# Evacuations in place, without temporaries, and attention masks made during the pooling stage

## The chip, the cores and the metric

The kernel runs on one core of a Trainium2 chip. The metric is the device time of one launch in microseconds (us). TensorE is called PE (its weight load PEld), VectorE DVE, ScalarE ACT, GpSimd POOL and SyncE SP. L12 is line 12 of the kernel whose profile is read; the same step has another line number in the changed kernel, since lines fall away.

## The reference

A decoder trunk of two layers on 256 tokens of width 2048, in float32. Layer 0 mixes tokens by causal means over windows of 2, 4, 8 and 16; layer 1 by causal attention with 16 heads, whose keys and values come from the stream after layer 0. Each mixer is followed by a gated feed-forward part with a causal convolution of width 3, and every part ends in a residual sum and a layer norm:

```python
def layer(h, mixer):
    h = layer_norm(ALPHA * h + mixer(h), ln1_g, ln1_b)
    u = h @ w_up                              # 2048 -> gate and value, D_FF each
    u = causal_conv3(u, conv_w, conv_b)
    g = silu(gate(u)) * value(u)
    return layer_norm(ALPHA * h + g @ w_down, ln2_g, ln2_b)
```

The three dilated branches of the attention (windows 128, 512 and 2048, strides 1, 4 and 16) see each other's keys several times. The kernel therefore weighs each pair of tokens with the number of branches that hold it. That count depends on the distance of the tokens alone: it is the mask `cnt`, and `negm` is a large negative number where the count is zero.

## The kernel before

Weights are streamed once. The work is cut into units, one for each weight block of 512 x 512, and a list gives their order. `run_units` goes through the list: before the matmuls of a unit it loads the raw block of the unit five further on (SP, `rawp`, three buffers) and splits the block three units further on into a high part `wh` (ACT cast, L82) and a low part `wl` (DVE subtraction, L83), each with four buffers. PE then multiplies wh and wl with the high and low parts of the activations, which stand for a product in float32. Blocks of the down projection are split in another way (L96, L97, L103 to L109) for a scheme of seven products with sums and differences of blocks; its outputs are added onto `ht` by DVE or by accumulating transfers that POOL issues (L271), and are transposed (L814) and moved on SP (L804).

The order of the instructions of each engine is that in which the code is written; `later(n, fn)` puts fn behind the matmuls n units on. So a step that waits holds up all that stands behind it on its engine.

An accumulator of PE has two halves of 256 columns, for the high and the low part of the activations, which have to be added. `evac` does that for an up group of four blocks of 128 channels: ACT copies the right half of a block to a temporary `ut` (L578; tag t1, three buffers), and DVE adds the left half and the temporary into `u` (L579). `u` comes from the tag t4 of the same pool, with four buffers, in which the convolution also keeps its results `c` and `a`. `qk_post` does the same for q and k of four heads (L978, L979; temporary `qt`, two buffers). Where the input of the layer norm is still folded into the product, `norm_evac` is used instead (L442 to L449), also with a temporary. The pooling stage has its own evacuation (L471, L473), which copies into the destination and adds in place there.

The stages follow each other in the list: pooling with its feed-forward part, then the attention with its own. The pools of temporaries `ffn0`, `attn` and `ffn1` stand in sequence. `masks` makes one of two blocks of `cnt` and `negm` (L1171 to L1178 on DVE, an iota on POOL, and for the first block two ACT copies, L1182). It runs 7 and 8 units into the attention stage, into buffers of the pool `attn`, with scratch from the tag t1, which the temporaries of q use too.

Of the kernel before, what the change touches and what calls it, by code (L numbers as in the profile page):

```python
# [17 lines left out]
T = 256  # L18
P = 128
# [9 lines left out]
NEG = -1e30  # L29
# [3 lines left out]
def trunk(ctx: ExitStack, tc: tile.TileContext, x, pool_w_in, pool_w_grp, pool_scale, pool_w_out,  # L33
# [86 lines left out]
    def later(n, fn):  # L120
        if n == 0:
            fn()
        else:
            pending.append([n, fn])
# [176 lines left out]
    ones4 = const.tile([P, P], F32R, name="ones4")  # L301
    epst = const.tile([P, 1], F32, name="epst")
    inv = const.tile([P, 1, 16], F32, name="inv")

    xsrcs = [lambda j=j: XC[j] for j in range(4)]
    psrcs = [lambda j=j: XP[j] for j in range(4)]
# [241 lines left out]
    def ffn(lay):  # L548
# [15 lines left out]
            return u  # L564

        def evac(ps, nb, mode):
            fp = pools["ffn"]
            u = pads()

            def tmp():  # L570
                return fp.tile([P, T], F32, name="ut", tag="t1", bufs=3)

            if mode == "x":
                norm_evac(ps, nb, tmp, lambda m: u[:, m, 2:])
                return u
            for m in range(nb):
                t = tmp()
                A.copy(t, ps[m][:, T:])  # L578
                V.tensor_tensor(u[:, m, 2:], ps[m][:, :T], t, OP.add)  # L579
            return u  # L580

        def conv(u, blk0, nb, then, quick=False):
# [378 lines left out]
    def qk_post(nm, hq):  # L961
        def post(ps):
            later(2 if hq == 0 and nm == "k" else 0, lambda: evac(ps))

        def evac(ps):
            ap = pools["attn"]
            o = ap.tile([P, 4, T], F32, name=nm, tag=nm)
            qk[nm] = o

            def tmp():  # L970
                return ap.tile([P, T], F32, name="qt", tag="t1", bufs=2)

            if hq == 0 and nm == "k":
                norm_evac(ps, 4, tmp, lambda m: o[:, m, :])
            else:
                for m in range(4):
                    t = tmp()
                    A.copy(t, ps[m][:, T:])  # L978
                    V.tensor_tensor(o[:, m, :], ps[m][:, :T], t, OP.add)  # L979
            if nm == "q":  # L980
                later(2, lambda: scores(hq, range(0, 2)))
                later(3, lambda: scores(hq, range(2, 4)))
                if hq < 3:
                    later(4, lambda: blocks(hq, (0, 1)))
                    later(7, lambda: blocks(hq, (2, 3)))
        return post

    def scores(hq, ms):
        ap = pools["attn"]
        for m in ms:  # L990
            ps = bank("s")
            q, k = qk["q"][:, m, :], qk["k"][:, m, :]
            PE.matmul(ps[:, 0:P], q[:, :P], k[:, :P], start=True, stop=True)
            PE.matmul(ps[:, P:3 * P], q[:, P:], k, start=True, stop=True)
            if m % 2 == 0:
                two = ap.tile([P, 2, 3, P], F32, name="p", tag="p", bufs=2)
            s = two[:, m % 2]
            sf, nf, cf = (t.rearrange("p a b -> p (a b)") for t in (s, ST["negm"], ST["cnt"]))
            V.scalar_tensor_tensor(sf, ps[:, :3 * P], scale, nf, op0=OP.mult, op1=OP.add)
            mx = ap.tile([P, 6], F32, name="mx", tag="mx", bufs=4)  # L1000
            parts = ((0, slice(0, P)), (1, slice(P, 3 * P)))
            for t, sl in parts:
                V.tensor_reduce(mx[:, t:t + 1], sf[:, sl], AX.X, OP.max)
            V.tensor_scalar(mx[:, 2:4], mx[:, 0:2], -1.0, None, op0=OP.mult)
            for t, sl in parts:
                A.activation(sf[:, sl], sf[:, sl], AF.Exp, bias=mx[:, 2 + t:3 + t])
            pr[hq, m] = (s, mx, two)
        for m in ms:
            s, mx, _ = pr[hq, m]
            sf, cf = (t.rearrange("p a b -> p (a b)") for t in (s, ST["cnt"]))  # L1010
            for t, sl in parts:
                V.scalar_tensor_tensor(sf[:, sl], sf[:, sl], 1.0, cf[:, sl], op0=OP.mult, op1=OP.mult,
                                       accum_out=mx[:, 4 + t:5 + t])
            V.reciprocal(mx[:, 0:2], mx[:, 4:6])
            for t, sl in parts:
                V.tensor_scalar(sf[:, sl], sf[:, sl], mx[:, t:t + 1], None, op0=OP.mult)
# [95 lines left out]
    with tc.tile_pool(name="pool", bufs=1) as pp:  # L1112
# [17 lines left out]
        def late_consts(l):  # L1130
# [16 lines left out]
            A.copy(t, ps.rearrange("p (j c) -> p j c", j=4)[:, :, :2 * NF])  # L1147
            cvec.append(t)

        later(2, lambda: late_consts(0))  # L1150
        later(4, lambda: late_consts(1))

# [4 lines left out]
        run_units(marks[1])  # L1157
    with tc.tile_pool(name="attn", bufs=1) as ap:
        pools["attn"] = ap
        for nm in ("cnt", "negm"):  # L1160
            ST[nm] = ap.tile([P, 3, P], F32, name=nm)

        def masks(i):
            two = ap.tile([P, 2, P], F32, name="dist", tag="t1", bufs=2)
            dist, fm = two[:, 0], two[:, 1]
            nc.gpsimd.iota(dist, pattern=[[-1, P]], base=P * (i == 1), channel_multiplier=1,
                           allow_small_or_imprecise_dtypes=True)
# [3 lines left out]
            V.tensor_copy(idist, dist)  # L1171
            V.tensor_scalar(cn, dist, float(P), None, op0=OP.is_le)
            for dil in (4, 16):
                V.tensor_scalar(im, idist, dil - 1, None, op0=OP.bitwise_and)
                V.tensor_copy(fm, im)
                V.scalar_tensor_tensor(cn, fm, 0.0, cn, op0=OP.is_equal, op1=OP.add)
            V.scalar_tensor_tensor(cn, dist, 0.0, cn, op0=OP.is_ge, op1=OP.mult)
            V.tensor_scalar(ST["negm"][:, i, :], cn, 0.0, NEG, op0=OP.is_equal, op1=OP.mult)  # L1178

            if i == 0:  # L1180
                for nm in ("cnt", "negm"):
                    A.copy(ST[nm][:, 2, :], ST[nm][:, 0, :])  # L1182

        for i in range(2):
# [34 lines left out]
```

## Time and profile before

| | us |
|---|---|
| median of 3 runs | 2051.32 (2048.59 to 2051.43) |
| the profiled execution | 2051.56 |
| span of the profiled execution | 2049.8 |
| PE busy | 2025.5 |
| DVE busy | 1684.2 |
| ACT busy | 1259.6 |
| POOL busy | 74.9 |

The profile is of one execution. The span goes from its first to its last instruction, and the launch's own time is 1.8 us more. Busy time is that in which an engine has at least one instruction under way. The idle time of an engine that is not the bottleneck costs nothing in itself; it counts where another engine waits for what comes late from it. All columns and groups below are in us unless marked ns.

### The profile page before, as it was taken

To read this page: it belongs to the slowest core of one execution; us is meant where nothing else is said; L and a number is where in the kernel's file an instruction comes from. 1 tells how busy PE (TensorE), PEld (TensorE's weight loads), DVE (VectorE), ACT (ScalarE), POOL (GpSimd) and SP (SyncE) were. 2 spreads that over 40 slices of the span, in tenths; PEclk is the share of its full clock that TensorE was granted. 3 is DMA by queue.
4 is the path that set the end of the run, shared out by engine and by line. 5 is a ranking of instruction groups with operands and counts; after the bars stand their busy time and mean duration, and the time that the engine had idled before them with its cause. 6 is when DMAs were issued, how large, how long until landed. Compare 5 with 4: busy or idle time off the path is not lost. (4 is left out here: it accounts for less than half of the span.)

```text
span 2049.8 us, 31251 instructions
## 1 busy us (share of the span) xinstructions
PE 2025.5 (99%) x12532; PEld 1809.4 (88%) x12532; DVE 1684.2 (82%) x2010; ACT 1259.6 (61%) x1691; POOL 74.9 (4%) x111
## 2 busy tenths in 40 slices
PE   9999999999999999999999999999999999999998
PEld 8899988899899989889888888998899988889987
DVE  6759876998889898889856657787889888989989
ACT  6545687666756686657544444477666677667663
POOL 2000000000000101000000000000001000100000
PEclk9999999999999999999999999999999999999999
DMA  8655467667656657775566554557666756666565
GB/s 263 213 190 186 169 211 202 191 194 235 196 190 201 202 190 210 211 231 170 167 218 191 173 180 165 185 185 221 187 199 185 227 181 208 205 216 197 184 206 185
DMA packets 278305, 405.92 MB, mean 198 GB/s; under 512 B 80414, under 2 KB 95668, under 8 KB 277904
## 3 DMA queue, kind: packets, MB, share of 16 engines
q1 hardware_dynamic: 266144, 389.72, 57.5%
q0 software_dynamic: 11584, 13.55, 4.4%
q8 instruction: 98, 1.61, 0.3%
q10 hardware_dynamic: 432, 0.66, 0.1%
q14 instruction: 47, 0.39, 0.1%
HBM read 380.01 MB, written 2.10 MB: 186 GB/s over the span
## 5 line engine op out<-in xcount | busy, mean ns | idle before, releaser
L165 PE MATMUL acc<-xc,wh 128*128 128x512 f32 x3264 | 1152.8, 396 | 1.2 <-DVE o L1064 1.2
L166 PE MATMUL acc<-xc,wl 128*128 128x256 f32 x3264 | 917.3, 281 | 5.3 <-DVE wl L83 5.1
L83 DVE TENSOR_TENSOR wl<-raw,wh 128x2048 fp32r<-128x2048 f32 (+2 forms) x318 | 687.5, 2168 | 259.1 <-ACT wh L82 258.7
L165 PEld LDWEIGHTS acc<-xc,wh 128*128 128x128 f32 x3264 | 615.9, 189 | 144.4 <-DVE o L1064 1.9
L82 ACT CAST wh<-raw 128x2048 fp32r<-128x2048 f32 (+2 forms) x318 | 573.7, 1810 | 201.2 <-PE acc L165 108.4
L166 PEld LDWEIGHTS acc<-xc,wl 128*128 128x128 f32 x3264 | 615.4, 189 | 9.2 <-DVE wl L83 8.5
L96 ACT CAST wh<-raw 128x1024 fp32r<-128x1024 f32 x116 | 121.9, 1053 | 156.8 <-DVE raw L107 133.4
L97 DVE TENSOR_TENSOR wl<-raw,wh 128x1024 fp32r<-128x1024 f32 x116 | 138.4, 1221 | 0.0
L103 ACT CAST wh<-raw 128x1024 fp32r<-128x1024 f32 x116 | 90.7, 832 | 35.6 <-DMA raw<-in_ffn_w_down_dram 21.3
L106 DVE TENSOR_TENSOR wl<-raw,wh 128x1024 fp32r<-128x1024 f32 x116 | 105.7, 952 | 2.6 <-ACT wh L103 2.2
L587 ACT ACTIVATE c<-u,cv 128x256 f32<-128x256 f32 x172 | 89.5, 593 | 24.6 <-DVE f L650 8.5
L578 ACT COPY ut<-acc 128x256 f32<-128x256 f32 x164 | 53.1, 372 | 81.6 <-DVE u L579 58.6
L228 PE MATMUL t<-wl,g 128*128 128x256 f32 x344 | 97.0, 282 | 0.0
L227 PE MATMUL t<-wh,g 128*128 128x256 f32 x344 | 97.0, 282 | 0.0
L229 PE MATMUL t<-wh,g 128*128 128x256 f32 x344 | 96.7, 281 | 0.0
L228 PE MATMUL s<-wl,xs 128*128 128x256 f32 x308 | 86.9, 282 | 3.8 <-DVE wl L97 3.8
L229 PE MATMUL s<-wh,xs 128*128 128x256 f32 x308 | 86.4, 280 | 0.0
L227 PE MATMUL s<-wh,xs 128*128 128x256 f32 x308 | 86.3, 280 | 0.0
L271 POOL DMA_DIRECT2D ht<-w x24 | 20.3, 847 | 1770.6 <-ACT wh L103 1034.8
L592 ACT ACTIVATE a<-u,cv 128x256 f32<-128x256 f32 x172 | 73.6, 501 | 12.3 <-DVE g L660 6.5
L592 ACT ACTIVATE u<-u,cv 128x256 f32<-128x256 f32 x172 | 73.5, 500 | 0.0
L109 DVE TENSOR_TENSOR raw<-raw 128x1024 f32<-128x1024 f32 x58 | 71.0, 1225 | 2.0
(278 smaller groups left out, 3433.8 us busy)
## 6 DMA issues: line engine op xcount, KB each, us to landing
raw<-in_ffn_w_up_dram SPq DMA_DIRECT2D x160, 1024.0 KB, 4.9
raw<-in_ffn_w_down_dram SPq DMA_DIRECT2D x80, 1024.0 KB, 5.1
raw<-in_pool_w_out_dram SPq DMA_DIRECT2D x16, 1024.0 KB, 5.0
raw<-in_shared_w_k_dram SPq DMA_DIRECT2D x16, 1024.0 KB, 5.1
raw<-in_attn_w_q_dram SPq DMA_DIRECT2D x16, 1024.0 KB, 5.4
raw<-in_shared_w_v_dram SPq DMA_DIRECT2D x16, 1024.0 KB, 5.6
raw<-in_attn_w_o_dram SPq DMA_DIRECT2D x16, 1024.0 KB, 5.0
raw<-in_pool_w_in_dram SPq DMA_DIRECT2D x12, 1024.0 KB, 5.5
```

The source lines that it names most:

```text
L82: A.copy(wh[i][:, s], r[:, s])
L83: V.tensor_tensor(wl[i][:, s], r[:, s], wh[i][:, s].bitcast(F32), OP.subtract)
L96: A.copy(h[:, :, n], r[:, :, n])
L97: V.tensor_tensor(l[:, :, n], r[:, :, n], h[:, :, n].bitcast(F32), OP.subtract)
L103: A.copy(h[:, k, n], r[:, k, n])
L106: V.tensor_tensor(l[:, k, n], r[:, k, n], h[:, k, n].bitcast(F32), OP.subtract)
L165: PE.matmul(ps[m], h[:, k, c], q[:, k, :, :T], start=st, stop=False)
L166: PE.matmul(ps[m][:, :T], l[:, k, c], q[:, k, 0, :T], start=False, stop=sp and not shifted)
L227: PE.matmul(to, xh, h[:, k, n], start=opens and kk == 0, stop=False)
L228: PE.matmul(to, xh, l[:, k, n], start=False, stop=False)
L229: PE.matmul(to, xl, h[:, k, n], start=False, stop=ends and kk == 1)
L592: A.activation(to[:, m, :], u[:, m, i:i + T], AF.Copy, scale=cv[:, i, j:j + 1])
```

## The change

The temporaries of `evac`, of q and k and of `norm_evac` are dropped: ACT copies the right half of the accumulator straight into the destination, and DVE adds the left half to it in place; in `norm_evac` DVE and ACT work in the destination. `cnt` and `negm` move to the pool of constants, and `masks` runs 9 and 10 units into the pooling stage, with scratch from two tags of the pool `lnp` that are free there.

```diff
@@ -301,6 +301,8 @@
     ones4 = const.tile([P, P], F32R, name="ones4")
     epst = const.tile([P, 1], F32, name="epst")
     inv = const.tile([P, 1, 16], F32, name="inv")
+    cnt = const.tile([P, 3, P], F32, name="cnt")
+    negm = const.tile([P, 3, P], F32, name="negm")
 
     xsrcs = [lambda j=j: XC[j] for j in range(4)]
     psrcs = [lambda j=j: XP[j] for j in range(4)]
@@ -436,17 +438,17 @@
         later(5, lambda: lo(3))
 
 
-    def norm_evac(ps, nb, tmp, dst):
+    def norm_evac(ps, nb, dst):
         wgb = lnp.tile([P, 4, 2], F32, name="wgb", tag="wgb", bufs=2)
         for m in range(nb):
             A.copy(wgb[:, m, :], ps[m][:, T:XW])
         for m0 in range(0, nb, 2):
-            ts = [(m, tmp()) for m in range(m0, min(nb, m0 + 2))]
+            ts = [(m, dst(m)) for m in range(m0, min(nb, m0 + 2))]
             for m, t in ts:
                 V.tensor_tensor(t, ps[m][:, :T], ST["rs"], OP.mult)
             for m, t in ts:
                 V.scalar_tensor_tensor(t, ST["mr"], wgb[:, m, 0:1], t, op0=OP.mult, op1=OP.subtract)
-                A.activation(dst(m), t, AF.Identity, scale=-1.0, bias=wgb[:, m, 1:2])
+                A.activation(t, t, AF.Identity, scale=-1.0, bias=wgb[:, m, 1:2])
 
 
     def turns(mark, n, nb):
@@ -564,19 +566,14 @@
             return u
 
         def evac(ps, nb, mode):
-            fp = pools["ffn"]
             u = pads()
 
-            def tmp():
-                return fp.tile([P, T], F32, name="ut", tag="t1", bufs=3)
-
             if mode == "x":
-                norm_evac(ps, nb, tmp, lambda m: u[:, m, 2:])
+                norm_evac(ps, nb, lambda m: u[:, m, 2:])
                 return u
             for m in range(nb):
-                t = tmp()
-                A.copy(t, ps[m][:, T:])
-                V.tensor_tensor(u[:, m, 2:], ps[m][:, :T], t, OP.add)
+                A.copy(u[:, m, 2:], ps[m][:, T:])
+                V.tensor_tensor(u[:, m, 2:], u[:, m, 2:], ps[m][:, :T], OP.add)
             return u
 
         def conv(u, blk0, nb, then, quick=False):
@@ -967,16 +964,12 @@
             o = ap.tile([P, 4, T], F32, name=nm, tag=nm)
             qk[nm] = o
 
-            def tmp():
-                return ap.tile([P, T], F32, name="qt", tag="t1", bufs=2)
-
             if hq == 0 and nm == "k":
-                norm_evac(ps, 4, tmp, lambda m: o[:, m, :])
+                norm_evac(ps, 4, lambda m: o[:, m, :])
             else:
                 for m in range(4):
-                    t = tmp()
-                    A.copy(t, ps[m][:, T:])
-                    V.tensor_tensor(o[:, m, :], ps[m][:, :T], t, OP.add)
+                    A.copy(o[:, m, :], ps[m][:, T:])
+                    V.tensor_tensor(o[:, m, :], o[:, m, :], ps[m][:, :T], OP.add)
             if nm == "q":
                 later(2, lambda: scores(hq, range(0, 2)))
                 later(3, lambda: scores(hq, range(2, 4)))
@@ -995,7 +988,7 @@
             if m % 2 == 0:
                 two = ap.tile([P, 2, 3, P], F32, name="p", tag="p", bufs=2)
             s = two[:, m % 2]
-            sf, nf, cf = (t.rearrange("p a b -> p (a b)") for t in (s, ST["negm"], ST["cnt"]))
+            sf, nf, cf = (t.rearrange("p a b -> p (a b)") for t in (s, negm, cnt))
             V.scalar_tensor_tensor(sf, ps[:, :3 * P], scale, nf, op0=OP.mult, op1=OP.add)
             mx = ap.tile([P, 6], F32, name="mx", tag="mx", bufs=4)
             parts = ((0, slice(0, P)), (1, slice(P, 3 * P)))
@@ -1007,7 +1000,7 @@
             pr[hq, m] = (s, mx, two)
         for m in ms:
             s, mx, _ = pr[hq, m]
-            sf, cf = (t.rearrange("p a b -> p (a b)") for t in (s, ST["cnt"]))
+            sf, cf = (t.rearrange("p a b -> p (a b)") for t in (s, cnt))
             for t, sl in parts:
                 V.scalar_tensor_tensor(sf[:, sl], sf[:, sl], 1.0, cf[:, sl], op0=OP.mult, op1=OP.mult,
                                        accum_out=mx[:, 4 + t:5 + t])
@@ -1147,27 +1140,14 @@
             A.copy(t, ps.rearrange("p (j c) -> p j c", j=4)[:, :, :2 * NF])
             cvec.append(t)
 
-        later(2, lambda: late_consts(0))
-        later(4, lambda: late_consts(1))
-
-        run_units(marks[0])
-    with tc.tile_pool(name="ffn0", bufs=4) as fp:
-        pools["ffn"] = fp
-
-        run_units(marks[1])
-    with tc.tile_pool(name="attn", bufs=1) as ap:
-        pools["attn"] = ap
-        for nm in ("cnt", "negm"):
-            ST[nm] = ap.tile([P, 3, P], F32, name=nm)
-
         def masks(i):
-            two = ap.tile([P, 2, P], F32, name="dist", tag="t1", bufs=2)
-            dist, fm = two[:, 0], two[:, 1]
+            both = lnp.tile([P, 4, T], F32, name="dist", tag="sq")
+            dist, fm = (both[:, j, :P] for j in range(2))
+            two = lnp.tile([P, 2, T], I32, name="idist", tag="fold2")
+            idist, im = two[:, 0, :P], two[:, 1, :P]
             nc.gpsimd.iota(dist, pattern=[[-1, P]], base=P * (i == 1), channel_multiplier=1,
                            allow_small_or_imprecise_dtypes=True)
-            itwo = ap.tile([P, 2, P], I32, name="idist", tag="t1", bufs=2)
-            idist, im = itwo[:, 0], itwo[:, 1]
-            cn = ST["cnt"][:, i, :]
+            cn = cnt[:, i, :]
             V.tensor_copy(idist, dist)
             V.tensor_scalar(cn, dist, float(P), None, op0=OP.is_le)
             for dil in (4, 16):
@@ -1175,14 +1155,23 @@
                 V.tensor_copy(fm, im)
                 V.scalar_tensor_tensor(cn, fm, 0.0, cn, op0=OP.is_equal, op1=OP.add)
             V.scalar_tensor_tensor(cn, dist, 0.0, cn, op0=OP.is_ge, op1=OP.mult)
-            V.tensor_scalar(ST["negm"][:, i, :], cn, 0.0, NEG, op0=OP.is_equal, op1=OP.mult)
-
+            V.tensor_scalar(negm[:, i, :], cn, 0.0, NEG, op0=OP.is_equal, op1=OP.mult)
             if i == 0:
-                for nm in ("cnt", "negm"):
-                    A.copy(ST[nm][:, 2, :], ST[nm][:, 0, :])
+                for t in (cnt, negm):
+                    A.copy(t[:, 2, :], t[:, 0, :])
 
         for i in range(2):
-            later(7 + i, lambda i=i: masks(i))
+            later(9 + i, lambda i=i: masks(i))
+        later(2, lambda: late_consts(0))
+        later(4, lambda: late_consts(1))
+
+        run_units(marks[0])
+    with tc.tile_pool(name="ffn0", bufs=4) as fp:
+        pools["ffn"] = fp
+
+        run_units(marks[1])
+    with tc.tile_pool(name="attn", bufs=1) as ap:
+        pools["attn"] = ap
         run_units(marks[2])
     with tc.tile_pool(name="ffn1", bufs=4) as fp:
         pools["ffn"] = fp
```

Where the steps land is seen in the order of instructions. First an evacuation in layer 0, on DVE and on ACT, before (u is the destination, acc the accumulator, raw the loaded block; numbers tell buffers of a name apart):

```order
L83 TENSOR_TENSOR wl_4501<-raw_4437,wh_4500 128x2048
L563 MEMSET u 128x4x2
L579 TENSOR_TENSOR u<-acc,ut 128x256 x4
L83 TENSOR_TENSOR wl_4551<-raw_4466,wh_4550 128x2048
L104 TENSOR_TENSOR raw_4498<-raw_4498 128x2x256
```

```order
L82 CAST wh_4500<-raw_4437 128x2048
L578 COPY ut<-acc 128x256 x4
L82 CAST wh_4550<-raw_4466 128x2048
L587 ACTIVATE c<-u,cv_590 128x256 x4
L103 CAST wh_4579<-raw_4498 128x4x256
```

And the same place with the change, DVE and ACT:

```order
L83 TENSOR_TENSOR wl_4499<-raw_4435,wh_4498 128x2048
L565 MEMSET u 128x4x2
L576 TENSOR_TENSOR u<-u,acc 128x256 x4
L83 TENSOR_TENSOR wl_4545<-raw_4464,wh_4544 128x2048
L104 TENSOR_TENSOR raw_4496<-raw_4496 128x2x256
```

```order
L82 CAST wh_4498<-raw_4435 128x2048
L575 COPY u<-acc 128x256 x4
L82 CAST wh_4544<-raw_4464 128x2048
L584 ACTIVATE c<-u,cv_592 128x256 x4
L103 CAST wh_4573<-raw_4496 128x4x256
```

Nothing has moved here; operands have changed. Second, DVE in the pooling stage ahead of the adds (pb is their destination) that end the second of its groups, before:

```order
L83 TENSOR_TENSOR wl_815<-raw_685,wh_814 128x2048
L83 TENSOR_TENSOR wl_857<-raw_742,wh_856 128x2048
L83 TENSOR_TENSOR wl_895<-raw_812,wh_894 128x2048
L83 TENSOR_TENSOR wl_933<-raw_854,wh_932 128x2048
L473 TENSOR_TENSOR pb_420<-pb_420,acc 128x256 x4
```

and with the change, the end of the first block of masks and what follows up to the second:

```order
L1156 SCALAR_TENSOR_TENSOR cnt<-dist,cnt 128x128
L1157 SCALAR_TENSOR_TENSOR cnt<-dist,cnt 128x128
L1158 TENSOR_SCALAR negm<-cnt 128x128
L83 TENSOR_TENSOR wl_950<-raw_856,wh_949 128x2048
L1151 CAST idist<-dist 128x128
L1152 TENSOR_SCALAR cnt<-dist 128x128
L1154 TENSOR_SCALAR idist<-idist 128x128
```

Ten steps now stand ahead of the fourth wl of the four, and ten between it and the adds. Third, DVE in the attention stage ahead of the first q, before, the end of the second block of masks:

```order
L1176 SCALAR_TENSOR_TENSOR cnt<-dist,cnt 128x128
L1177 SCALAR_TENSOR_TENSOR cnt<-dist,cnt 128x128
L1178 TENSOR_SCALAR negm<-cnt 128x128
L979 TENSOR_TENSOR q<-acc,qt 128x256 x4
L83 TENSOR_TENSOR wl_9725<-raw_9605,wh_9724 128x2048
```

and with the change:

```order
L450 SCALAR_TENSOR_TENSOR k<-rm,wgb,k 128x256 x2
L83 TENSOR_TENSOR wl_9546<-raw_9437,wh_9545 128x2048
L83 TENSOR_TENSOR wl_9584<-raw_9486,wh_9583 128x2048
L972 TENSOR_TENSOR q<-q,acc 128x256 x4
L83 TENSOR_TENSOR wl_9631<-raw_9543,wh_9630 128x2048
```

The add of q now follows straight behind two wl. The order of PE and of SP is the same in both kernels; on POOL the two iotas stand ahead of all accumulating transfers.

More of the change, by code (lines that the diff above doesn't have):

```diff
@@ L1148, in late_consts, with masks @@
             cvec.append(t)
+        def masks(i):
+            both = lnp.tile([P, 4, T], F32, name="dist", tag="sq")
+            dist, fm = (both[:, j, :P] for j in range(2))
+            two = lnp.tile([P, 2, T], I32, name="idist", tag="fold2")
+            idist, im = two[:, 0, :P], two[:, 1, :P]
+            nc.gpsimd.iota(dist, pattern=[[-1, P]], base=P * (i == 1), channel_multiplier=1,
+                           allow_small_or_imprecise_dtypes=True)
+            cn = cnt[:, i, :]
+            V.tensor_copy(idist, dist)
+            V.tensor_scalar(cn, dist, float(P), None, op0=OP.is_le)
+            for dil in (4, 16):
+                V.tensor_scalar(im, idist, dil - 1, None, op0=OP.bitwise_and)
+                V.tensor_copy(fm, im)
+                V.scalar_tensor_tensor(cn, fm, 0.0, cn, op0=OP.is_equal, op1=OP.add)
+            V.scalar_tensor_tensor(cn, dist, 0.0, cn, op0=OP.is_ge, op1=OP.mult)
+            V.tensor_scalar(negm[:, i, :], cn, 0.0, NEG, op0=OP.is_equal, op1=OP.mult)
+            if i == 0:
+                for t in (cnt, negm):
+                    A.copy(t[:, 2, :], t[:, 0, :])
+        for i in range(2):
+            later(9 + i, lambda i=i: masks(i))
         later(2, lambda: late_consts(0))
@@ L1159, in trunk @@
         pools["attn"] = ap
-        for nm in ("cnt", "negm"):
-            ST[nm] = ap.tile([P, 3, P], F32, name=nm)
-        def masks(i):
-            two = ap.tile([P, 2, P], F32, name="dist", tag="t1", bufs=2)
-            dist, fm = two[:, 0], two[:, 1]
-            nc.gpsimd.iota(dist, pattern=[[-1, P]], base=P * (i == 1), channel_multiplier=1,
-                           allow_small_or_imprecise_dtypes=True)
-            itwo = ap.tile([P, 2, P], I32, name="idist", tag="t1", bufs=2)
-            idist, im = itwo[:, 0], itwo[:, 1]
-            cn = ST["cnt"][:, i, :]
[L1171 to L1180, printed above, removed]
-                for nm in ("cnt", "negm"):
-                    A.copy(ST[nm][:, 2, :], ST[nm][:, 0, :])
-        for i in range(2):
-            later(7 + i, lambda i=i: masks(i))
         run_units(marks[2])
```

## The prediction

> **What bounds the kernel now.** I read the head of the page first, then the waits of TensorE (PE), then its waits in windows, and then the timeline of the two engines that prepare its operands.
>
> ```profile
> span 2049.8 us, 31251 instructions
> PE 2025.5 (99%) x12532; PEld 1809.4 (88%) x12532; DVE 1684.2 (82%) x2010; ACT 1259.6 (61%) x1691; POOL 74.9 (4%) x111
> ```
>
> PE is busy for 99% of the span. The change leaves its instructions and their order alone, so all that can be won is the time in which PE stands still. The waits of PE over the whole span (total, times, longest, in us) show how much that is, and for whom PE waits:
>
> ```profile
> PE acc L166 <- DVE wl L83: 5.1, 8, 2.0
> PE s L228 <- DVE wl L97: 3.8, 4, 1.5
> PE t L229 <- DVE xs3Q L660: 1.9, 1, 1.9
> PE acc L168 <- ACT wh L82: 1.9, 1, 1.9
> PE acc L165 <- DVE o L1064: 1.2, 1, 1.2
> ```
>
> Two rows, 8.9 us together, are waits for wl, the low half of a weight block, which VectorE (DVE) makes from the raw block and the high half wh that ScalarE (ACT) casts before it. The wait for L82 (1.9) stands in the first 10 us, which the change does not touch. The other waits for wl are placed by windows: the first row is 600 to 780 us, the next two 780 to 870, then one of 1700 to 1900 and two of 1900 to 1980; the L1064 row above is the only one of 1000 to 1080.
>
> ```profile
> PE acc L166 <- DVE wl L83: 1.3, 3, 0.7
> PE s L228 <- DVE wl L97: 2.6, 2, 1.5
> PE acc L166 <- DVE wl L83: 2.4, 2, 2.0
> PE acc L166 <- DVE wl L83: 1.0, 2, 0.8
> PE s L228 <- DVE wl L97: 0.9, 1, 0.9
> PE acc L166 <- DVE wl L83: 0.5, 1, 0.5
> ```
>
> So wl comes late in two stretches, the end of each layer's feed-forward part: 6.3 us in layer 0, 2.4 us in layer 1. What delays DVE there? The waits of ACT hold one suspect, and the timeline around 658 us shows one evacuation of an up group (start, duration, engine, line; in brackets the idle time before and its releaser; first ACT, then DVE):
>
> ```profile
> ACT ut L578 <- DVE u L579: 58.6, 27, 3.8
> ```
>
> ```profile
> 657.88 0.91 ACT L578 COPY ut<-acc 128x256 f32<-128x256 f32 x3
> 660.74 0.38 ACT L578 COPY ut<-acc 128x256 f32<-128x256 f32 x1 [1.95 <-DVE u L579]
> 661.01 1.92 ACT L82 CAST wh<-raw 128x2048 fp32r<-128x2048 f32 x1
> ...
> 658.02 2.29 DVE L83 TENSOR_TENSOR wl<-raw,wh 128x2048 fp32r<-128x2048 f32 x1 [0.58 <-ACT wh L82]
> 660.24 0.41 DVE L579 TENSOR_TENSOR u<-acc,ut 128x256 f32<-128x256 f32 x1
> 660.57 1.07 DVE L579 TENSOR_TENSOR u<-acc,ut 128x256 f32<-128x256 f32 x3
> 662.96 2.29 DVE L83 TENSOR_TENSOR wl<-raw,wh 128x2048 fp32r<-128x2048 f32 x1 [1.32 <-ACT wh L82]
> ```
>
> ACT makes three copies and stops: there are three buffers ut and four blocks. The fourth copy waits until DVE has done its first add (660.65), and DVE gets to that only after a wl of 2.29 us. Behind the fourth copy stands the next L82 cast, which ends at 662.93, and DVE, done with its adds at 661.64, stands idle for 1.32 us until that cast is there. The loop costs DVE 1.32 us an evacuation, where DVE is what PE waits for.
>
> **The change part by part.** Evacuation of up groups. Without ut the four ACT copies go straight into four parts of u and need none of the adds. They would run from 657.88 for 4 x 0.30 = 1.2 us, the cast behind them from 659.1 to 661.0, and DVE would find it ready at 661.64. So each evacuation of four blocks gives DVE back the bracket of the wl behind it. The add itself now reads u and the accumulator rather than the accumulator and ut. That form is in the trace, in the pooling stage (L473; by line and form: total, mean ns):
>
> ```profile
> L579 DVE TENSOR_TENSOR u<-acc,ut 128x256 f32<-128x256 f32 x164 | 58.0, 414 | 1.8 <-ACT ut L578 1.8
> L473 DVE TENSOR_TENSOR pb<-pb,acc 128x256 f32<-128x256 f32 x12 | 4.5, 414 | 1.9 <-ACT pb L471 1.9
> ```
>
> Both take 414 ns, so the add costs the same. How far do the brackets reach PE? The same bracket stands behind these evacuations before the stalls of layer 0, the first three in full:
>
> ```profile
> 736.31 2.29 DVE L83 TENSOR_TENSOR wl<-raw,wh 128x2048 fp32r<-128x2048 f32 x1 [1.31 <-ACT wh L82]
> 752.52 2.29 DVE L83 TENSOR_TENSOR wl<-raw,wh 128x2048 fp32r<-128x2048 f32 x1 [1.31 <-ACT wh L82]
> 784.60 2.29 DVE L83 TENSOR_TENSOR wl<-raw,wh 128x2048 fp32r<-128x2048 f32 x1 [1.31 <-ACT wh L82]
> 817.38 1.76 DVE L83 TENSOR_TENSOR wl<-raw,wh 128x1536 fp32r<-128x1536 f32 x1 [0.88 <-ACT wh L82]
> 819.83 1.25 DVE L814 STREAM_TRANSPOSE hb<-ht 128x1024 f32<-128x1024 f32 x1 [0.70 <-DMA ht<-u]
> ```
>
> With the one at 662.96 that is 4 x 1.31 = 5.2 us of DVE time against 6.3 us of stalls. The last row shows why the one at 817.38 counts nothing: the next DVE step waits for a transfer anyhow. I take 5.2 us for layer 0. The lower bound is the 1.3 us of 600 to 780, which lie straight behind evacuations; the upper one is all 6.3. In layer 1 the evacuations behind 1740 us are of the same kind, with more brackets than stalls, so I take the 2.4 us of stalls there; the last of them hang on a cast that waits for PE,
>
> ```profile
> 1958.90 2.24 ACT L96 CAST wh<-raw 128x1024 fp32r<-128x1024 f32 x2 [0.97 <-PE acc L165]
> ```
>
> so that no more than 0.97 us can come at that place, and the 0.9 and 0.5 there may not both go: 2.3 us, with 1.0 as the lower bound. The upper bound adds the 1.9 us of L229 (a later step of the same chain) and what follows it, the PE clock (windows: length, busy of PE, PEld, DVE, ACT, POOL, then granted clock, DMA share, GB/s; first 3 us behind a stall of 2.0 us in layer 0, then 3 us behind that of 1.9):
>
> ```profile
> 835.00:838.00 3.00, 3.00 (x19) 2.58 (x18) 2.52 (x4) 1.72 (x3) 0.00 (x0) 1.00 0.86 292
> 1985.10:1988.10 3.00, 3.00 (x16) 3.00 (x15) 3.00 (x6) 2.78 (x6) 0.00 (x0) 0.50 0.36 88
> ```
>
> Behind the second, PE ran at half clock for 3 us, which costs 1.5 us; behind the first it did not. The Trainium skill's page "TensorE: Matmul & The Clock Gate" (section "What's actually happening") gives half clock only after an idle window of about 3.4 us; by that rule a stall of 1.9 us would cost nothing more, and the upper bound would be 1.5 us smaller. The row at 1985 speaks against it. Upper bound of layer 1: 2.4 + 1.9 + 1.5 = 5.8 us.
>
> Evacuation of q and k. Same edit, four blocks and two buffers. Here the masks of the attention stage make it worse: they stand on DVE ahead of the first q evacuation (first and last step of one of two blocks of ten; the copy and the cast that wait behind it; what PE's only stall here hangs on):
>
> ```profile
> 987.07 0.22 DVE L1171 CAST idist<-dist 128x128 int32<-128x128 f32 x1
> 989.24 0.23 DVE L1178 TENSOR_SCALAR negm<-cnt 128x128 f32<-128x128 f32 x1
> 995.43 0.37 ACT L978 COPY qt<-acc 128x256 f32<-128x256 f32 x1 [3.83 <-DVE dist L1175]
> 997.27 3.71 ACT L82 CAST wh<-raw 128x2048 fp32r<-128x2048 f32 x2
> 1035.92 0.74 DVE L1064 TENSOR_TENSOR o<-o 128x256 fp32r<-128x256 f32 x2
> ```
>
> Each block is 2.4 us (987.07 to 989.47). Without them and without the wait of 3.83 us, DVE and ACT are 3 to 4 us earlier at 1000; the stall of 1.2 us at 1036 hangs on the DVE step of the last row, 36 us on, behind softmax, transfers and transposes. I take all 1.2 us; bounds 0 and 1.2.
>
> Masks in the pooling stage. The 20 DVE steps (4.8 us), two ACT copies and two POOL iotas come back there. On POOL the iotas stand behind the small constant loads and ahead of all accumulating transfers, which start hundreds of us later, so nothing queues behind them. On DVE the first block falls between two wl, the second between a wl and the adds that free the banks of the next unit (DVE, ACT, then PE's opening of that unit):
>
> ```profile
> 82.78 2.29 DVE L83 TENSOR_TENSOR wl<-raw,wh 128x2048 fp32r<-128x2048 f32 x1 [3.28 <-ACT wh L82]
> 87.00 0.42 DVE L473 TENSOR_TENSOR pb<-pb,acc 128x256 f32<-128x256 f32 x1 [0.93 <-ACT pb L471]
> ...
> 80.84 1.91 ACT L82 CAST wh<-raw 128x2048 fp32r<-128x2048 f32 x1 [3.66 <-PE acc L165]
> ...
> 92.11 0.40 PE L165 MATMUL acc<-xc,wh 128*128 128x512 f32 x1
> ```
>
> The first block fits into the 3.28 us in which DVE idles, but the two ACT copies wait for its end (82.78 - 3.28 + 2.4 = 81.9) and push the cast from 80.84 to about 82.1, and so the wl from 82.78 to about 84.0. It ends at 86.3, the second block at 88.7, and the last of four adds at about 90.4 at the latest instead of 87.4. PE opens the unit at 92.11: 1.7 us of cover is left, and the cost is 0. Gone, the cover would cost some tenths of a us. Bounds: 0 and 4.8 us, if all steps lay on the path.
>
> Sum: 5.2 + 2.3 + 1.2 - 0 = 8.7 us. The profiled execution took 2051.56 us, 0.24 above the median 2051.32, so 2042.9 of its kind and 2042.6 as a median.
>
> **The rivals.** A, only stalls that lie straight behind evacuations go. From 780 us on the path runs through loads of down blocks and through transfers (the 0.70 before L814 at 819.83 is one such wait); if those set the pace, an earlier DVE only waits longer for them. Left are 1.3 in layer 0, 1.0 in layer 1 and 1.2 at 1036: 3.5 us, 2047.8. For it speaks that row; against it that DVE at 784.60 waits for ACT and not for a transfer.
>
> B, nothing comes of it: DVE ahead by a few us is stopped by ACT casts that wait for PE to free a wh buffer (3.66 us before 80.84 is such a wait), and every stall forms again; the 1.2 at 1036 goes or stays. 2050.1 to 2051.3.
>
> C, slower: the wait moves from ut to u. ACT's first copy now needs a whole free u of the ring t4, which also holds c, a and what the gate makes, four buffers in all; before, only DVE's add needed it, behind work of DVE's own. If the ring is freed by the DVE convolution steps, the copy stalls in place, and the L82 behind it. Two such steps of some 1.2 us (the transposing step of 1.25 at 819.83 has the same 1024 elements a row) cost 2.5 us where 1.31 is won: 1.2 us lost at each of the 7 evacuations with DVE on the path in layer 0 (624 to 817), 8.4 us in all: 2059.7. It decides as soon as the copy waits for over 1.31 us. The order of instructions speaks against it: of 41 evacuations the first copy gets a new wait in only four. The Trainium skill's "Perfetto Trace Analysis" (section "Optimization Strategy") says that the same gap repeating over a stretch can mean too little room for the next tile; the repeated 1.31 us agrees, and by that rule giving up three buffers should lengthen the gap, which is this rival.
>
> **How the numbers follow.** The forecast and what lies near it (over 4.1 us won): 0.70. A: 0.12. B: 0.08. C, or a late pooling stage of the size of its upper bound: 0.10. A measurement of this kernel tells 0.2%, 4.1 us, from no change; A and B lie within that. So faster 0.70, same 0.20, slower 0.10. Low end: 6.3 + 5.8 + 1.2 = 13.3 us won, 2038.0. High end: 2051.3, the end of B; beyond it lies C with 0.10.
>
> **What would show it.** Right: ACT's wait for u L579 is gone (58.6 us to near 0), the brackets of 1.31 us behind evacuations too, no PE wait for wl between 600 and 780, less than 2 us of 5 between 780 and 870, and none for L1064; PE opens the unit after the masks at 92 us without a gap. A: stalls at 828 to 863 as now. B: ACT's L82 waits for PE grow by what the ut waits lose, and PE's waits stay. C: a new wait of the first copy on the convolution's DVE or ACT steps (L592 and L593 before), and longer brackets. The forecast is wrong if PE's waits in layer 0 lose less than 3 us, or if a wait appears that is not among the rows above.

## The result, and the profile after

| | before | with the change |
|---|---|---|
| median of 4 runs, us | 2051.38 (2048.59 to 2053.28) | 2037.69 (2037.24 to 2040.06) |
| profiled execution, us | 2051.56 | 2040.06 |

The ratio is 0.9938, 95% interval 0.9922 to 0.9953: faster by 0.6%, 13.7 us between the medians. The change's profiled execution was its longest, so the traces account for 11.5 us. The median lies 0.3 us below the low end of the forecast range; 5.0 us more were won than the 8.7 forecast.

The head of the page and five rows of PE's waits, with the change (total, times, longest, us; line numbers are those of the changed kernel, which differ from those before by a few lines). Not shown are waits that are there in both kernels, such as those for w and u near 867 us (1.1 and 0.7 us):

```profile
span 2038.3 us, 31218 instructions
PE 2022.3 (99%) x12532; PEld 1808.7 (89%) x12532; DVE 1682.8 (83%) x2010; ACT 1262.9 (62%) x1691; POOL 75.1 (4%) x111
```

```profile
PE s L228 <- DVE wl L97: 1.9, 3, 1.4
PE t L229 <- DVE xs3Q L657: 1.3, 1, 1.3
PE t L239 <- DVE wl L83: 1.1, 1, 1.1
PE acc L166 <- DVE wl L83: 0.7, 2, 0.5
PE shift L364 <- DVE S L347: 0.2, 1, 0.2
```

The waits of L166 for wl fell from 5.1 to 0.7 us; the row of L165 waiting for the attention output `o` is not there any more. Between 600 and 780 us, and between 1700 and 1900, PE waits for nothing. ACT's two rows that matter:

```profile
ACT wh L82 <- PE acc L165: 132.4, 58, 3.7
ACT u L575 <- PE acc L166: 51.3, 56, 1.0
```

The wait for DVE's add (58.6 us before) is gone. What stands before the copies now is PE itself: ACT is there first and waits at most 1.0 us for the accumulator. That is also the answer to rival C: no copy waits for a free u. And the evacuation that the prediction showed at 658 us (ACT, then DVE):

```profile
653.89 1.90 ACT L82 CAST wh<-raw 128x2048 fp32r<-128x2048 f32 x1
655.70 1.19 ACT L575 COPY u<-acc 128x256 f32<-128x256 f32 x4
656.78 1.92 ACT L82 CAST wh<-raw 128x2048 fp32r<-128x2048 f32 x1
...
655.82 2.29 DVE L83 TENSOR_TENSOR wl<-raw,wh 128x2048 fp32r<-128x2048 f32 x1 [0.58 <-ACT wh L82]
658.05 0.41 DVE L576 TENSOR_TENSOR u<-u,acc 128x256 f32<-128x256 f32 x1
658.38 1.08 DVE L576 TENSOR_TENSOR u<-u,acc 128x256 f32<-128x256 f32 x3
659.37 2.28 DVE L83 TENSOR_TENSOR wl<-raw,wh 128x2048 fp32r<-128x2048 f32 x1
```

Four copies run without a pause, the cast behind them ends at 658.70, and the second wl follows the adds with no bracket: the 1.32 us of DVE are back.

PE runs the same 12532 matmuls in the same order in both, so the start of each can be compared. The lead of the change over the kernel before, by place (time in the kernel before, lead in us, worked out from the two traces):

```
 100     0.0
 640-642 +0.95   678-680 +0.50   721-724 +0.42   766-768 +0.64      2.6
 826-828 +1.39   830-834 +2.27                                      6.3
 843     -0.39   856-859 +0.18   869-872 -0.37   872-877 -1.56      4.2
 898-902 +0.99   1034-1038 +1.29                                    6.6
 1748-50 +1.05   1785-88 +0.47   1873-75 +0.32   1947 +0.29         8.8
 1960-63 +1.18   1964-67 +0.73   1980-89 +0.74                     11.5
```

All of it comes in steps, at stalls and where PE's clock is halved (872-877 with the change, 1980-89 before); between them the kernels run in step.

### The profile page after: what moved, and what is told of

Read it like the earlier page. It is cut to its first block, busy times and chain, and to the rows that moved or that the text cites. A ratio compares the mean times of both kernels' runs of the same rounds, so it can differ in the third digit from the quotient of the medians.

```text
span 2038.3 us, 31218 instructions
## 1 busy us (share of the span) xinstructions
PE 2022.3 (99%) x12532; PEld 1808.7 (89%) x12532; DVE 1682.8 (83%) x2010; ACT 1262.9 (62%) x1691; POOL 75.1 (4%) x111
## 3 DMA queue, kind: packets, MB, share of 16 engines
q8 instruction: 98, 1.61, 0.3%
## 5 line engine op out<-in xcount | busy, mean ns | idle before, releaser
L165 PE MATMUL acc<-xc,wh 128*128 128x512 f32 x3264 | 1152.1, 396 | 0.0
L166 PE MATMUL acc<-xc,wl 128*128 128x256 f32 x3264 | 915.8, 281 | 0.5 <-DVE wl L83 0.5
L83 DVE TENSOR_TENSOR wl<-raw,wh 128x2048 fp32r<-128x2048 f32 (+2 forms) x318 | 687.6, 2167 | 243.5 <-ACT wh L82 240.5
L165 PEld LDWEIGHTS acc<-xc,wh 128*128 128x128 f32 x3264 | 615.8, 189 | 143.5 <-DVE o L1057 0.6
L82 ACT CAST wh<-raw 128x2048 fp32r<-128x2048 f32 (+2 forms) x318 | 574.4, 1811 | 218.4 <-PE acc L165 132.4
L166 PEld LDWEIGHTS acc<-xc,wl 128*128 128x128 f32 x3264 | 615.3, 189 | 1.3 <-DVE wl L83 0.8
L97 DVE TENSOR_TENSOR wl<-raw,wh 128x1024 fp32r<-128x1024 f32 x116 | 138.4, 1221 | 0.0
L228 PE MATMUL t<-wl,g 128*128 128x256 f32 x344 | 96.7, 281 | 0.0
L229 PE MATMUL t<-wh,g 128*128 128x256 f32 x344 | 96.3, 280 | 0.0
L228 PE MATMUL s<-wl,xs 128*128 128x256 f32 x308 | 86.1, 280 | 1.9 <-DVE wl L97 1.9
L575 ACT COPY u<-acc 128x256 f32<-128x256 f32 x164 | 54.2, 373 | 51.3 <-PE acc L166 51.3
L229 PE MATMUL s<-wh,xs 128*128 128x256 f32 x308 | 85.9, 279 | 0.0
```

Of the source, the lines that this page charges most:

```text
L82: A.copy(wh[i][:, s], r[:, s])
L83: V.tensor_tensor(wl[i][:, s], r[:, s], wh[i][:, s].bitcast(F32), OP.subtract)
L97: V.tensor_tensor(l[:, :, n], r[:, :, n], h[:, :, n].bitcast(F32), OP.subtract)
L165: PE.matmul(ps[m], h[:, k, c], q[:, k, :, :T], start=st, stop=False)
L166: PE.matmul(ps[m][:, :T], l[:, k, c], q[:, k, 0, :T], start=False, stop=sp and not shifted)
L228: PE.matmul(to, xh, l[:, k, n], start=False, stop=False)
```

## The experiments

Each kernel was timed in five rounds beside the kernel before on the same chip (e3 in eleven, e9 once). The medians there were 2052.05 us for e1, e3, e4 and e5, 2051.40 for e6 to e9, and 2051.56 for e10 and e11.

**e1, up groups alone.**

```diff
             for m in range(nb):
-                t = tmp()
-                A.copy(t, ps[m][:, T:])
-                V.tensor_tensor(u[:, m, 2:], ps[m][:, :T], t, OP.add)
+                A.copy(u[:, m, 2:], ps[m][:, T:])
+                V.tensor_tensor(u[:, m, 2:], u[:, m, 2:], ps[m][:, :T], OP.add)
```

> Only the up groups are evacuated in place; q, k, the norm's evacuation and the masks are as before. Theory (the wait of ACT's fourth copy on three buffers is what makes wl late): all of layer 0's and layer 1's gain is there, about 10 us of the 11.5 between the profiled executions, and only the 1.2 us stall at 1036 stays: 2040 to 2042. Rival (what was won from 1000 us on comes from the masks leaving the attention stage, which shifts layer 1): only layer 0's part, 2045 to 2047, and the stalls at 1749 and 1962 are as before.

2039.93 us, ratio 0.9939 (0.9926 to 0.9951). Its lead over the kernel before has the same steps as the change's from 640 to 834 us (+0.95, +0.50, +0.42, +0.64, +1.39, +2.27) and from 1747 to 1967 (+1.05, +0.47, +0.32, +0.29, +1.18, +0.73). Only the stall behind the attention is still there, in PE's waits of e1:

```profile
PE acc L165 <- DVE o L1063: 1.2, 1, 1.2
```

So the up groups carry nearly all of the gain, in both layers, and the rival falls: layer 1 does not need the masks to move.

**e4, the fourth block alone.** Three blocks still go through ut, with its three buffers.

```diff
-                t = tmp()
+                t = tmp() if m < 3 else u[:, m, 2:]
```

> The kernel before, with one difference: the fourth block of an up group is copied straight into u, the first three still through the three buffers ut. Theory (buffers, not temporaries as such): the fourth copy no longer waits, so the same as with all four in place, within 1.5 us: 2040 to 2042. Rival (three temporaries fewer to fill and the operands' places matter by themselves, a share for each block): a quarter of the gain, 2048 to 2049.

2040.48 us, ratio 0.9941 (0.9927 to 0.9954), not to be told from e1. ACT at the same evacuation in e4:

```profile
655.02 0.91 ACT L578 COPY ut<-acc 128x256 f32<-128x256 f32 x3
655.84 0.37 ACT L578 COPY u<-acc 128x256 f32<-128x256 f32 x1
656.11 1.92 ACT L82 CAST wh<-raw 128x2048 fp32r<-128x2048 f32 x1
```

The first three copies run as before; the fourth no longer waits, and within the spread of the runs that is the whole effect. It is a matter of places for four blocks, not of temporaries as such.

**e5, two buffers.**

```diff
-                return fp.tile([P, T], F32, name="ut", tag="t1", bufs=3)
+                return fp.tile([P, T], F32, name="ut", tag="t1", bufs=2)
```

> The kernel before with two buffers ut instead of three. Theory: the third copy waits for DVE's first add and the fourth for its second, so the cast behind them ends about 0.4 us later and DVE's idle time behind an evacuation grows from 1.3 to 1.7 us; at some 4 evacuations on the path in each layer that is 3 us more: 2053 to 2056. Rival (the number of buffers does not matter, only whether the add is in place): 2051.4.

2063.75 us, ratio 1.0052 (1.0039 to 1.0064): slower by 11.7 us where I expected 3; so the rival falls. One evacuation in e5 (ACT, then DVE):

```profile
662.66 0.70 ACT L578 COPY ut<-acc 128x256 f32<-128x256 f32 x2 [2.23 <-DVE u L579]
663.26 1.91 ACT L82 CAST wh<-raw 128x2048 fp32r<-128x2048 f32 x1
...
662.15 0.41 DVE L579 TENSOR_TENSOR u<-acc,ut 128x256 f32<-128x256 f32 x1
663.06 0.76 DVE L579 TENSOR_TENSOR u<-acc,ut 128x256 f32<-128x256 f32 x2 [0.16 <-ACT ut L578]
665.20 2.29 DVE L83 TENSOR_TENSOR wl<-raw,wh 128x2048 fp32r<-128x2048 f32 x1 [1.38 <-ACT wh L82]
```

From the first add to the wl behind it are 3.05 us, where the kernel before took 2.72 (660.24 to 662.96): 0.33 us more for each evacuation, near the 0.4 expected. That PE lost far more than 4 + 4 times that is a miss in the count. Its trace shows PE late already at 481 and 637 us, ahead of the first stall of the kernel before. With 41 evacuations in all, 0.33 us each would be 13.5 us; so DVE's lateness seems to add up over many more evacuations than those in sight of a stall. That reading was not tested further. Part of the miss is PE's clock: this trace has half clock in four stretches of 3.41 us (from 837, 878, 1755 and 1991 us), the kernel before in one (from 1985). The one from 1755 alone held 3.07 us of PE's work, so about 1.5 us were lost in it.

**e3, q and k alone.**

```diff
-                    t = tmp()
-                    A.copy(t, ps[m][:, T:])
-                    V.tensor_tensor(o[:, m, :], ps[m][:, :T], t, OP.add)
+                    A.copy(o[:, m, :], ps[m][:, T:])
+                    V.tensor_tensor(o[:, m, :], o[:, m, :], ps[m][:, :T], OP.add)
```

> Only q and k are evacuated in place; the up groups, the norm's evacuation and the masks are as before, the masks still ahead of the first q. Theory: the copies of q no longer wait, but DVE's 4.8 us of masks stay ahead of its adds, so between nothing and the 1.2 us stall at 1036: 2050 to 2051.4. Rival (the masks do not matter, the temporaries of q do): the stall at 1036 goes all the same, 2050.

2051.78 us, ratio 0.9996 (0.9988 to 1.0005). By time nothing can be told. The trace tells: the stall at 1036 is gone, with a step of +1.28 us in the lead, though the masks are still there. The rival's condition holds: the masks ahead of q do not keep the stall. ACT in e3:

```profile
992.21 1.18 ACT L977 COPY q<-acc 128x256 f32<-128x256 f32 x4
993.26 3.74 ACT L82 CAST wh<-raw 128x2048 fp32r<-128x2048 f32 x2
```

The pair of casts starts at 993.26, against 997.27 before: 4 us won by the copies alone. What was won at 1036 was lost in steps of 0.3 to 0.7 at other places, mostly near 830, where this execution has a longer wait for wl (1.81 us) and half clock behind it (828.9 to 832.3).

**e6, the masks left in the attention stage, and e7, q and k left with temporaries.** e6 is the change with the masks where and when they were; e7 is the change with this taken back:

```diff
-                    A.copy(o[:, m, :], ps[m][:, T:])
-                    V.tensor_tensor(o[:, m, :], o[:, m, :], ps[m][:, :T], OP.add)
+                    t = tmp()
+                    A.copy(t, ps[m][:, T:])
+                    V.tensor_tensor(o[:, m, :], ps[m][:, :T], t, OP.add)
```

> All evacuations in place as in the change, but the masks are made where they were, in the attention stage. Theory (the evacuation of q and k is what frees the cast behind it; the place of the masks is worth nothing by itself): the stall near 1036 is gone as with the masks moved, and the time is that of the change, 2037 to 2039.5. Rival (DVE's 4.8 us of masks ahead of the first q add delay the path to that stall): the stall of 1.2 us is back, 2039 to 2041.

> The change, but q and k are evacuated through two buffers qt as before; the masks are in the pooling stage. Theory: the wait of the copies of q for DVE's adds is back and with it some or all of the 1.2 us stall near 1036: 2038 to 2041. Rival (either part alone takes the stall away, since taking the masks off DVE gives more than the 1.2 us): no stall there, 2037 to 2039.5.

2039.39 us, ratio 0.9935 (0.9923 to 0.9948), and 2039.65 us, 0.9939 (0.9925 to 0.9952). Neither trace has a wait of PE near 1030. In e7 the wait of q's copies for DVE's adds is there (2.61 us at 984), and the stall is not. So either part takes that stall away and both together take no more: e6's theory and e7's rival. For the time of this kernel the move of the masks is worth nothing that can be measured. What it changes is where memory goes: two masks of three blocks of 128 float32 columns take 3 KB a partition in lasting memory, as much as the three buffers ut of 256 columns took in the feed-forward pools.

**e8, no accumulating transfers between 780 and 870 us.** Their sums are left out there.

```diff
-                ST["onto"] = [(y0, w), (y1[:, :256], u), (y1[:, 256:], u5)]
+                ST["onto"] = [] if by_dma == "none" else [(y0, w), (y1[:, :256], u), (y1[:, 256:], u5)]
...
-                         seven=sv, early=early_post(c, not last))
+                         seven=sv, early=early_post(c, "none" if lay == 0 and n == 2 else not last))
```

> The change without the accumulating transfers that POOL issues in the third down part of layer 0 (780 to 870 us): their sums are not added onto ht, and only there. Theory (the stalls that the change left near 853 to 857, 1.4 and 0.5 us, come through transfers: the transposing step waits for the accumulation and the raw block loaded beside it takes 6.5 instead of 4.9 us): both stalls go, and 2 to 3 us with them, 2035 to 2036.5. Rival (DVE's own work sets them): they stay, 2037.5 to 2038.5.

2037.89 us, ratio 0.9928 (0.9915 to 0.9940); the interval overlaps the change's, so the 2 to 3 us are not shown by time. The trace shows 1.9 of them: the first two rows are the last transposing step in the change and in e8, the third all of PE's wait for L97 in e8.

```profile
845.08 1.25 DVE L811 STREAM_TRANSPOSE hb<-ht 128x1024 f32<-128x1024 f32 x1 [2.05 <-issue]
```

```profile
841.98 1.24 DVE L811 STREAM_TRANSPOSE hb<-ht 128x1024 f32<-128x1024 f32 x1
```

```profile
PE s L228 <- DVE wl L97: 0.3, 1, 0.3
```

Without the accumulation DVE does not stop for 2.05 us, PE's stall of 1.35 us at 853 goes, that of 0.46 at 856 shrinks to 0.19, and e8 gains 1.9 us on the change between 850 and 857. These stalls are the part that rival A named.

**e9, the change once more.**

> The changed kernel once more, for one more profiled execution. The first had half clock of PE for some 3 us behind the stalls of 1.1 and 0.7 us near 867 and lost 1.6 us there; the kernel before had the same stalls without it. Theory (the clock drop is not set by the program alone): it may be absent here with the same stalls, and then the execution is about 1.5 us shorter than the 2040.06 of the first. Rival (the change brings it about): it is there again.

2038.77 us, and half clock was there again, over the whole 3 us, as the rival says. By itself this does not decide, since e1, e5 and e8 have it too, and e4, e6, e7, e10 and e11 do not; taken with the other traces it has a pattern, which is in the last section.

**e10 and e11, two tries at what is left.** e10 issues the moves of h from POOL (`moves` gets the engine as an argument); e11 turns an order round.

```diff
-        moves(hf, to)
+        moves(hf, to, nc.gpsimd)
```

```diff
-                for v, src in vs:
+                for v, src in reversed(vs):
                     V.tensor_tensor(v[1], src, v[0].bitcast(F32), OP.subtract)
```

> The change, and the 16 small moves after each transposing step of layer 0's last down part (h from hb) are issued by POOL instead of SP, where they stand ahead of the loads of raw blocks. Theory (the stalls left near 853 to 868 come through loads that start late, behind those moves, and run beside them): raw blocks there are issued up to 4 us earlier, the waits for wl before 866 (1.4, 0.5 and 0.3 us) shrink, and with them the half clock behind 868: 1 to 4 us less than the change, 2034 to 2037. Rival (the moves delay the accumulations on POOL's queue, or the loads stay as slow beside them): the same as the change or up to 2 us more, 2037 to 2040.

> The change, and DVE makes the low parts of the sums for a seven-product block in reverse order, xs3Q ahead of xs. Theory (PE's wait of 1.3 us for xs3Q near 1972 is one for DVE's order alone): xs3Q is there 1.0 us earlier, but the wl of the same unit (L97) still comes behind all of them, so the wait moves to L228 and 0 to 0.5 us are won: 2037 to 2038. Rival (the wait goes as a whole): 1.3 us less than the change.

2038.42 us, ratio 0.9938 (0.9926 to 0.9951), and 2038.35 us, 0.9939 (0.9925 to 0.9952): neither can be told from the change. In e10 one load was issued 8 us earlier (842.1 us, against 850.3 with the change), but the loads near 855 still took 5.8 to 7.4 us and the stalls at 852 and 856 stayed (1.70 and 0.46 us); the wait of 0.26 us at 865 went, and the one for w behind it fell from 1.08 to 0.29. In e11 the wait moved, as expected (PE's waits in e11):

```profile
PE s L228 <- DVE wl L97: 2.7, 2, 1.5
PE t L229 <- DVE xs3Q L657: 0.3, 1, 0.3
```

L229 waits 1.0 us less, L228 at the same place 0.9 us more (1.22 where it was 0.28). No version here beats the change.

## Why the prediction was right or wrong

**The mechanism was right.** The bracket behind each evacuation went, as worked out, with the add at its old price (412 ns). e1 and e4 show that it is the fourth copy's wait, with nothing else that the times could tell; e5 shows the other direction.

**The masks' new place: right.** The forecast had the delayed wl at 84.0, the second block at 86.3 to 88.7, the adds done by 90.4 and PE unmoved at 92.11. DVE (first block's start and end, wl, second block's end, adds) and PE with the change:

```profile
79.42 0.22 DVE L1151 CAST idist<-dist 128x128 int32<-128x128 f32 x1
81.58 0.23 DVE L1158 TENSOR_SCALAR negm<-cnt 128x128 f32<-128x128 f32 x1
83.98 2.29 DVE L83 TENSOR_TENSOR wl<-raw,wh 128x2048 fp32r<-128x2048 f32 x1 [2.17 <-ACT wh L82]
88.36 0.23 DVE L1158 TENSOR_SCALAR negm<-cnt 128x128 f32<-128x128 f32 x1
88.50 1.40 DVE L475 TENSOR_TENSOR pb<-pb,acc 128x256 f32<-128x256 f32 x4
...
92.10 0.40 PE L165 MATMUL acc<-xc,wh 128*128 128x512 f32 x1
```

The adds end at 89.90, 2.2 us ahead of PE, and the lead at 100 us is 0.0.

**q and k: right in size, with one cause too many.** 1.2 was forecast, 1.29 measured. The forecast took the masks and the copies' wait away together; e3 shows that ending the copies' wait is enough, e7 that moving the masks is enough too.

**Layer 0: the sum right by accident.** 5.2 us were forecast; the lead at 1030 us is 5.3. It is made of other parts: +6.3 up to 834 us, all the stalls there, then 1.1 lost again up to 902. Lost were 0.8 in two new waits for wl (0.31 us at 837, 0.26 at 865) and 1.6 in half clock; regained were 0.2 at 856 and 1.0 at 900, where PE waits for the layer norm's sum S (L345, 1.22 us before; L347, 0.22 with the change), a wait that no term of the forecast holds. The stalls at 853 and 856 stayed, as rival A said, and e8 shows that they are mostly the accumulations' doing. So A holds for that place, with 1.8 us, not for all from 780 on: those at 828 and 833 went.

**Layer 1: the term that was too small.** 2.3 us were forecast, 4.9 measured (lead 6.6 to 11.5). Two steps failed. The first is taking the gaps in PE's waits as the price of a stall. A stall costs more than its gap, as the xs3Q wait in the change shows on PE:

```profile
1970.45 0.28 PE L228 MATMUL t<-wl,xs3S 128*128 128x256 f32 x1
1972.05 0.39 PE L229 MATMUL t<-wh,xs3Q 128*128 128x256 f32 x1 [1.32 <-DVE xs3Q L657]
1972.27 0.28 PE L227 MATMUL t<-wh,xs3S 128*128 128x256 f32 x1
1972.39 0.28 PE L228 MATMUL t<-wl,xs3S 128*128 128x256 f32 x1
```

Matmuls of 256 columns start every 0.12 us but last 0.28, so the gap, counted from the end of the one before, leaves out 0.16 us; and the first one after it keeps the next waiting for 0.22 instead of 0.12. 1.60 - 0.12 + 0.10 = 1.58 us were lost for a gap of 1.32. The steps in the lead agree: +0.95 for a gap of 0.67, +0.50 for 0.23, +1.39 for 1.11, each 0.28 more. For the four stalls that the 2.3 us were added up from that is 1.1 us. Two more delays of PE, at 1874 and 1947 us, show gaps of under 0.05 us and so stand in no row of waits, but cost 0.3 us each; they went too. The second step is leaving out the end of the chain (L229, 1.9 us, taken into the upper bound alone): it shrank to 1.3, and the half clock behind it went, +0.74 together, though a new wait of 1.1 us (L239) came behind it.

**The rest.** The range's low end summed gaps in the same way and missed the median by 0.3 us. Two of the signs that the prediction named went against it: between 780 and 870 us 2.4 us of waits for wl are left where it said less than 2, and a wait appeared that is in none of its rows (L239, 1.1 us). Between the profiled execution of the change and its median lie 2.4 us. Set beside e11's trace, which has no half clock there, the half clock at 872 to 877 cost 1.6 us, of which 0.7 came back at the wait for S (0.88 us in e11), and the wait at 837, which e11 does not have either, cost 0.6: 1.5 us in all. Whether the median execution was like e11 in this no trace shows. Rival B did not come: ACT waits longer for PE (132.4 for 108.4 us), as it said, but PE's waits for wl (L83 and L97) fell from 8.9 to 3.7 us.

## What to carry to other kernels

Where an engine hands pieces through fewer buffers than it makes in one go, look at what is queued behind the piece that waits, not at the wait: here 1.95 us of idle ACT were harmless in themselves, and the cast behind them was what PE waited for. One more place to write to is enough, and if the destination is free already it is the cheapest one. When pricing stalls of PE, compare starts of matmuls, not the gaps of the waits: each of these short gaps cost 0.28 us more than it showed.

## What the hardware showed

PE's clock halved for about 3 us behind 867 us in some executions and not in others. There are three gaps there (wl, w and u). Their sum in us in all twelve traces and the granted clock of the 3 us from the last gap on are:

```
e10 0.98 1.00    e6 1.57 1.00    before 1.77 1.00    e7 1.77 1.00
e11 1.78 1.00    e3 1.92 1.00    e4     1.96 1.00
e8  2.02 0.61    after 2.03 0.72   e5   2.03 0.67    e1 2.33 0.64    e9 2.57 0.50
```

Two of the rows, of e4 and of e8 (length, busy of PE, PEld, DVE, ACT and POOL, granted clock, DMA share, GB/s):

```profile
866.96:869.96 3.00, 2.93 (x15) 2.37 (x16) 3.00 (x4) 2.53 (x4) 1.93 (x3) 1.00 0.51 154
```

```profile
865.24:868.24 3.00, 2.92 (x9) 2.34 (x10) 3.00 (x4) 1.85 (x4) 0.00 (x0) 0.61 0.27 106
```

Up to 1.96 us of idle time nothing happened at this place; from 2.02 us on the clock fell, and 1.5 to 1.6 us were lost there. But it is no rule of the sum: near 1983, gaps of 1.61 and 0.28 us brought 0.53 in e7, while 2.06 and 0.28 left 1.00 in e3, and the single gap of 1.99 us at 833 in the kernel before left 1.00. Three traces also have half clock behind stalls elsewhere: e3 from 829, e6 from 853, and e5 from 837 and 1755 us.

What else decides can be read from the traces. In every one of the twelve the granted clock changes only at whole multiples of 3.413 us from its first change: in the kernel before, for instance, at 5.16 us and then, 580 and 581 stretches on, at 1984.89 and 1988.31. Where this grid lies differs between executions (first change at 5.16 us in the kernel before, 5.82 with the change, 7.32 in e9). Counted by these stretches, what matters is PE's idle time inside one of them. With the change, one stretch holds most of the gaps for w and u, and the next one has half clock (first two rows); in e4 the boundary at 865.46 cuts through the gap for w, and the two stretches share the idle time (last three rows):

```profile
865.98:869.40 3.42, 1.87 (x7) 1.20 (x8) 3.28 (x8) 2.67 (x5) 0.24 (x1) 1.00 0.69 234
869.40:872.81 3.41, 3.41 (x12) 2.86 (x11) 3.41 (x2) 0.17 (x1) 2.35 (x3) 0.50 0.71 107
```

```profile
862.04:865.46 3.42, 2.34 (x12) 1.60 (x10) 3.42 (x3) 2.23 (x3) 0.00 (x0) 1.00 1.02 383
865.46:868.87 3.41, 2.47 (x11) 1.71 (x12) 3.27 (x7) 2.75 (x4) 0.84 (x2) 1.00 0.67 244
868.87:872.28 3.41, 3.41 (x21) 2.97 (x20) 3.41 (x4) 0.62 (x3) 1.75 (x3) 1.00 0.89 127
```

Between 20 and 2025 us the twelve traces have twelve stretches of half clock. Each comes behind a stretch in which PE stood still for 1.55 to 2.37 us, and no stretch with more than 1.72 us is without one; between 1.55 and 1.72 us both happen, and why is open (the ends of matmuls are modelled in the profile). The cases above fit: the 1.99 us of the kernel before are cut into 0.27 and 1.72, the 2.06 and 0.28 of e3 into 0.96 and 1.37, and 1.66 of e7's 1.89 fall into one stretch. So whether the same stalls cost half clock depends in part on where an execution lies on this grid. This was read from the traces afterwards; no run was made to test it. The Trainium skill's "TensorE: Matmul & The Clock Gate" (section "What's actually happening") puts the fall behind at least one idle window of about 3.4 us. The length agrees with the 3.41 us here; but the stretches ahead of the falls were idle for 1.55 to 2.37 us of it, not throughout, and the measurement decides.
